# Raw weights of two quads in one tile: splits of 1024 columns, one accumulating transfer for both, and the output projection's transposes behind their unit

## The chip, the cores and the metric

The kernel runs on one core of a Trainium2 chip. The metric is the device time of one launch in microseconds (us), lower is better. The engines are called PE (TensorE: matmuls; PEld are its weight loads), DVE (VectorE), ACT (ScalarE), POOL (GpSimd) and SP (SyncE). Each runs its own instructions in order and waits for others by semaphores; transfers are issued by SP's and POOL's queues and land later.

## The reference

One layer of a hybrid decoder, for 256 positions of width 2048, all in float32. Cut to what matters here:

```python
def swiglu(h, w_gate, w_up, w_down):
    return (jax.nn.silu(h @ w_gate) * (h @ w_up)) @ w_down
...
        x = x + 0.5 * swiglu(rmsnorm(x, ffn1_norm[l]), ffn1_w_gate[l], ffn1_w_up[l], ffn1_w_down[l])
        h = rmsnorm(x, mix_norm[l])
        a_q, a_k, a_v, m_q, m_k, m_v, m_o, m_i, m_f = jnp.split(h @ w_in[l], split_idx, axis=-1)
...
        y_b = hm * jax.nn.sigmoid(m_o)
        x = x + jnp.concatenate([y_a, y_b], axis=-1) @ w_out[l]
        x = x + 0.5 * swiglu(rmsnorm(x, ffn2_norm[l]), ffn2_w_gate[l], ffn2_w_up[l], ffn2_w_down[l])
    return rmsnorm(x, final_norm)
```

Between them stand a differential attention (`y_a`) and an mLSTM (`hm`), both small. The FFN's inner width is 5632. Nearly all the time goes into `x @ w` with weights that are read once.

## The kernel before

**Products.** A float32 product is made of three matmuls of a faster, rounded type (fp32r). Each raw weight tile is split: ACT casts it to `wh` (L131), DVE subtracts that from the raw values to give the remainder `wl` (L132). The activations are split likewise. `mms` then issues, for each job, `wh` by the high part (L178) and `wh` by the low part (L179), and behind all jobs of the list `wl` by the high part (L181). Tiles `wh` and `wl` come from the pool `wsp`, four of each, so that ACT and DVE can run up to four tiles ahead of PE; splits have a high priority (AHEAD) and their order among themselves is the program's.

**Units.** `Paired` computes two output chunks of 512 columns, with weights `wa` and `wb`, in one unit. Of the contraction's 2048 (in tiles of 128 rows) the first `ns` "quads", each of two row tiles by two chunks, are multiplied by a scheme with seven products in place of eight; the remaining rows (`rest`) go by `plain` products, one tile of 128x1024 each. Quads are taken two at a time (`twos`). A quad's raw tile has three slots: one row tile of `wa` in slot 0 and both of `wb` in slots 1 and 2. The unit's stages are:

- `leading`: for each pair of quads it loads the raw tiles (L420 for `wa`, L205 for `wb`), splits slot 0 and multiplies (`part`, A1), and then DVE forms sums in place (L453). One pair later comes `second_sum`: the split and product of S1, and then slot 0 += slot 2. That sum is an accumulating transfer issued by POOL (L469), one for each quad; for the last of `twos`, and in units with `by_dma` off or three quads or fewer, it is a DVE addition (L471).
- `sums`: for each pair, the split and product of slot 0 (S2), then POOL adds the quad's second row of `wa` to it, which `late` has loaded through SP (L506, one transfer for each quad), and `bare` splits and multiplies the late tile itself. Then the same for S3 from slot 1.
- `second`: `both` (slots 0 and 2 of a quad, 128x1024 in one split) and the plain rows of `wa`; `third`: the plain rows of `wb`. `third` of a unit is run by `Chain` amid the next unit's `leading`.

Gate and up projections have `ns` = 5, in 20 units of both FFNs (pairs 2, 2, 1, so that two pairs of them take the transfer L469, four transfers a unit); the mixer's have 3 or 4, the down projections 3 or 2 with `by_dma` off, the output projection 3. Raw tiles of quads come from the pool `wr` (five tiles of one quad), plain and late ones from `wrp`.

In the split of a pair, each quad is split by itself, the two going to halves of one `wh` and one `wl`:

```python
                    for i, src in enumerate(srcs):
                        made = split_weights(src, t[0][:, i, :], t[1][:, i, :])
```

**Output projection.** Its input is `yT`, made by `y_transposes` (L1064): PE transposes `ya` (attention, in `weighted`) and `yb` (mLSTM, in `gate_out`) into `tr`, and ACT and DVE split them into `xt` or `xs`. The work is queued in `side` (one piece is run at each step, by `aside`) or in `pending` (run by `flush`). `second(gently=True)` is used in the first of the two output-projection units (c = 0): it runs one piece of `pending` at each step.

Program order, priorities and the tiles that come free set the order on each engine; the order of PE's matmuls in an FFN is the program's.

## Time and profile before

| what | value |
| --- | --- |
| median of 3 runs | 1776.93 us (1776.9 to 1777.61) |
| profiled execution, its own time | 1777.38 us |
| its span | 1775.3 us |
| granted TensorE clock | 0.999 |
| PE busy | 1758.5 us (99%) |
| DVE busy | 1605.0 us (90%) |
| ACT busy | 1263.6 us (71%) |
| POOL busy | 417.2 us (24%) |
| DMA moved | 427.08 MB, mean 241 GB/s |

A row of a timeline gives the start in us from the span's start, the duration in us, the engine, the line, the operation, what it writes and reads, the shape and how many stand in the row; in brackets the time for which the engine had been idle before, and what ended that. Where several instructions stand in one row, the duration is that from the first one's start to the last one's end. A row of groups ends in the busy time, the mean duration in ns, and the idle time just before with what ended most of it. A row of waits reads: who waited, at which line, for what; us in total, times, the longest one.

### The profile page before, as it was taken

What the parts mean: (1) busy time and instruction counts of PE and PEld (TensorE: products, weight loads), DVE (VectorE), ACT (ScalarE), POOL (GpSimd) and SP (SyncE); (2) the same over time, 40 slices, a digit from 0 to 9 for tenths busy, and PEclk for the clock granted to TensorE, in tenths of its full rate; (3) what the DMA queues carried; (4) which work ended last, traced back from release to release, by engine and by line L of the source; (5) the groups of instructions that cost most, each with busy time, mean ns of one, the idle gap of its engine ahead of it and who ended that gap; (6) DMA issues with size and microseconds to landing.
All of it is one profiled execution on the core that took longest, in us unless ns stands there. A gap on an engine that the chain in (4) does not pass through costs nothing. (4 is left out here: it accounts for less than half of the span.)

```text
span 1775.3 us, 24424 instructions
## 1 busy us (share of the span) xinstructions
PE 1758.5 (99%) x7942; PEld 1437.3 (81%) x7942; DVE 1605.0 (90%) x2168; ACT 1263.6 (71%) x1931; POOL 417.2 (24%) x614
## 2 busy tenths in 40 slices
PE   9999999999999999999999999999999999999998
PEld 7888888788888888987888788888888788888786
DVE  6989998999999999897788899999998999999998
ACT  7666676777677768776676677776676777677765
POOL 0022332332233311111121101122332333223310
PEclk9999999999999999999999999999999999999999
DMA  9787997998799876576776578897998999799874
GB/s 344 255 252 211 257 275 244 249 288 267 212 256 273 261 237 206 181 232 203 218 208 188 166 226 221 243 278 227 247 266 268 234 286 265 231 249 270 242 263 125
DMA packets 153296, 427.08 MB, mean 241 GB/s; under 512 B 17392, under 2 KB 18448, under 8 KB 152912
## 3 DMA queue, kind: packets, MB, share of 16 engines
q0 software_dynamic: 74192, 191.68, 42.8%
q1 hardware_dynamic: 77824, 231.76, 38.4%
q10 hardware_dynamic: 1152, 2.09, 0.3%
q8 instruction: 62, 1.02, 0.2%
q14 instruction: 66, 0.54, 0.1%
HBM read 349.56 MB, written 2.10 MB: 198 GB/s over the span
## 5 line engine op out<-in xcount | busy, mean ns | idle before, releaser
L131 ACT CAST wh<-raw 128x512 fp32r<-128x512 f32 (+2 forms) x865 | 587.1, 707 | 276.2 <-PE acc L179 84.6
L132 DVE TENSOR_TENSOR wl<-raw,wh 128x512 fp32r<-128x512 f32 (+2 forms) x865 | 661.6, 793 | 92.9 <-ACT wh L131 90.0
L132 DVE TENSOR_TENSOR wl<-rawp,wh 128x1024 fp32r<-128x1024 f32 (+3 forms) x316 | 373.9, 1197 | 25.8 <-ACT wh L131 21.4
L131 ACT CAST wh<-rawp 128x1024 fp32r<-128x1024 f32 (+3 forms) x316 | 322.5, 1033 | 60.1 <-PE acc L179 30.4
L178 PE MATMUL acc<-wh,xs 128*128 128x512 f32 (+2 forms) x924 | 358.6, 389 | 0.7 <-ACT us L477 0.5
L179 PE MATMUL acc<-wh,xs 128*128 128x512 f32 (+2 forms) x924 | 356.9, 387 | 0.0
L181 PE MATMUL acc<-wl,xs 128*128 128x512 f32 (+2 forms) x924 | 309.9, 389 | 1.2 <-DVE wl L132 1.1
L506 POOL DMA_DIRECT2D raw<-late x172 | 149.0, 1021 | 397.1 <-DVE wl L132 341.7
L178 PE MATMUL acc<-wh,xt 128*128 128x512 f32 (+2 forms) x592 | 228.7, 387 | 0.2 <-ACT wh L131 0.2
L178 PE MATMUL accn<-wh,xt 128*128 128x512 f32 (+1 forms) x576 | 227.6, 398 | 0.6 <-ACT accn L477 0.4
L179 PE MATMUL acc<-wh,xt 128*128 128x512 f32 (+2 forms) x592 | 227.8, 386 | 0.0
L179 PE MATMUL accn<-wh,xt 128*128 128x512 f32 (+1 forms) x576 | 224.0, 391 | 0.5
L453 DVE TENSOR_TENSOR raw<-raw 128x1024 f32<-128x1024 f32 (+1 forms) x172 | 206.6, 1216 | 0.1
L181 PEld LDWEIGHTS acc<-wl,xs 128*128 128x128 f32 x924 | 172.5, 188 | 41.5 <-DVE wl L132 7.2
L178 PEld LDWEIGHTS acc<-wh,xs 128*128 128x128 f32 x924 | 173.6, 188 | 36.1 <-ACT us L477 1.2
L179 PEld LDWEIGHTS acc<-wh,xs 128*128 128x128 f32 x924 | 173.6, 188 | 34.4 <-DVE xs L132 0.3
L181 PE MATMUL acc<-wl,xt 128*128 128x512 f32 (+2 forms) x592 | 165.3, 387 | 0.3
L181 PE MATMUL accn<-wl,xt 128*128 128x512 f32 (+1 forms) x576 | 161.3, 389 | 0.0
L178 PE MATMUL accn<-wh,xs 128*128 128x512 f32 (+1 forms) x392 | 153.2, 392 | 1.4 <-ACT wh L131 1.3
L179 PE MATMUL accn<-wh,xs 128*128 128x512 f32 (+1 forms) x392 | 151.9, 388 | 0.1
L469 POOL DMA_DIRECT2D raw<-raw x86 | 73.6, 873 | 307.0 <-DVE wl L132 293.7
L181 PE MATMUL accn<-wl,xs 128*128 128x512 f32 (+1 forms) x392 | 136.1, 389 | 0.1
(229 smaller groups left out, 2135.1 us busy)
## 6 DMA issues: line engine op xcount, KB each, us to landing
rawp<-in_wd_dram SPq DMA_DIRECT2D x88, 512.0 KB, 5.3
raw<-late POOLq DMA_DIRECT2D x170, 256.0 KB, 5.2
raw<-in_wu_dram POOLq DMA_DIRECT2D x80, 512.0 KB, 7.9
rawp<-in_wu_dram SPq DMA_DIRECT2D x74, 512.0 KB, 5.2
rawp<-in_wg_dram SPq DMA_DIRECT2D x70, 512.0 KB, 5.1
raw<-in_wd_dram POOLq DMA_DIRECT2D x44, 512.0 KB, 7.4
rawp<-in_win_dram SPq DMA_DIRECT2D x44, 512.0 KB, 4.6
raw<-raw POOLq DMA_DIRECT2D x86, 256.0 KB, 3.6
```

The costliest lines, as they stand in the source:

```text
L131: return (nc.scalar.copy(hi, src), nc.vector.tensor_tensor(out=lo, in0=src, in1=hi.bitcast(F32), op=ALU.subtract))
L132: nc.vector.tensor_tensor(out=lo, in0=src, in1=hi.bitcast(F32), op=ALU.subtract))
L178: nc.tensor.matmul(acc, lh, rh, start=first, stop=False, skip_group_check=on)
L179: nc.tensor.matmul(acc, ll, rh, start=False, stop=False, skip_group_check=on)
L181: nc.tensor.matmul(acc, lh, rl, start=False, stop=last, skip_group_check=on)
L453: nc.vector.tensor_tensor(out=raw[:, 0:2, :], in0=raw[:, 0:3:2, :], in1=raw[:, 1:2, :].to_broadcast([P, 2, n]), op=ALU.add)
L469: nc.gpsimd.dma_start(raw[:, 0, :], raw[:, 2, :], accum_op=ALU.add)
L506: nc.gpsimd.dma_start(self.raws[j][:, 0, :], lates[-1][1][:, i, :], accum_op=ALU.add)
```

## The change

- The pool `wr` holds tiles of two quads (`raw2`, two buffers) and of one quad (`raw1`, one buffer) in place of five tiles of one quad; the bytes are the same. `load` brings both quads' rows of `wa` in one transfer (512 KB) and each quad's of `wb` in one.
- A pair is split in one cast and one subtraction of 1024 columns. Its `wh` and `wl` stand where they stood.
- Slot 0 += slot 2 is one accumulating transfer of 512 KB for both quads (L478), and so is the addition of the late rows (L512); where DVE does the sum it is one instruction for both (L480).
- `mms` keeps its newest matmul, and in the first output-projection unit a piece of `pending` is issued behind that matmul (`tc.issue_after`). For the first attention head an empty piece goes into `side` ahead of its transposes, so that transposes of all heads run one step later.
- Spare loads (some plain tiles of the first unit) share one `raw2` tile.

The number of matmuls does not change, nor their order in the FFNs.

```diff
-    wr = ctx.enter_context(tc.tile_pool(name="wr", bufs=5))
+    wr = ctx.enter_context(tc.tile_pool(name="wr", bufs=2))
...
+    newest = []
     def mms(jobs):
...
-            nc.tensor.matmul(acc, lh, rl, start=False, stop=last, skip_group_check=on)
+            newest[:] = [nc.tensor.matmul(acc, lh, rl, start=False, stop=last, skip_group_check=on)]
...
+    def raw_tile(quads, n):
+        tag, bufs = ("raw2", 2) if quads == 2 else ("raw1", 1)
+        return wr.tile([P, quads, 3, n], F32, tag=tag, name=nm(tag), bufs=bufs)
...
-    def load(self, j):
+    def load(self, js):
...
-                self.queue.dma_start(raw[:, 0, :], self.wa[k // LK][:, k % LK, :])
-                load_pair(raw[:, 1:3, off:], self.wb, k, self.queue)
+                self.queue.dma_start(raw[:, :, 0, :], self.wa[k // LK][:, row:row + 2 * len(js) - 1:2, :])
+                for q in range(len(js)):
+                    load_pair(raw[:, q, 1:3, off:], self.wb, k + 2 * q, self.queue)
...
-    def split_two(self, srcs):
+    def split_two(self, src):
             with tc.high_priority(offset=AHEAD):
-                t = pair_tiles(wsp, "w", [P, 2, self.n])
-                if len(srcs) == 1 and len(srcs[0].shape) == 3:
-                    made = split_weights(srcs[0], *t)
-                else:
-                    for i, src in enumerate(srcs):
-                        made = split_weights(src, t[0][:, i, :], t[1][:, i, :])
-                splits.append(made)
+                t = [x[:, 0:src.shape[1], :] for x in pair_tiles(wsp, "w", [P, 2, self.n])]
+                splits.append(split_weights(src, *t))
             return t
...
-            t = self.split_two([self.raws[j][:, slot, :] for j in js])
+            t = self.split_two(self.twin[js[0]][:, :, slot, :])
...
-                        nc.gpsimd.dma_start(raw[:, 0, :], raw[:, 2, :], accum_op=ALU.add)
+                    nc.gpsimd.dma_start(raw[:, :, 0, :], raw[:, :, 2, :], accum_op=ALU.add)
...
-                    for i, j in enumerate(js):
-                        nc.gpsimd.dma_start(self.raws[j][:, 0, :], lates[-1][1][:, i, :], accum_op=ALU.add)
+                    nc.gpsimd.dma_start(self.twin[js[0]][:, :, 0, :], lates[-1][1][:, 0:len(js), :],
+                                        accum_op=ALU.add)
...
-                flush(1 if gently else 0 if i % 2 else None)
+                if gently:
+                    with tc.issue_after(newest[0].ins):
+                        flush(1)
+                else:
+                    flush(0 if i % 2 else None)
...
+        if h == 0:
+            side.append(lambda: None)
         side.append(functools.partial(y_transposes, [y[:, hb, :] for hb in range(NT)], 2 * h, gatt))
```

What this does to the order of instructions is seen in one gate-and-up unit on DVE, from the S1 split of its first pair to the S2 split of its second. Before (`raw_429`, `raw_430` are the first pair, `raw_436`, `raw_437` the second, `raw_442` the fifth quad; `rawp` is a plain tile of the unit before, `wl_456` and `wl_459` are S2):

```order
L132 TENSOR_TENSOR wl_441_2239<-raw_430_2183,wh_440_2238 128x512
L132 TENSOR_TENSOR wl_444_2256<-raw_442_2252,wh_443_2255 128x512
L132 TENSOR_TENSOR wl_446_2264<-raw_436_2218,wh_445_2263 128x512
L453 TENSOR_TENSOR raw_442_2252<-raw_442_2252 128x1024
L132 TENSOR_TENSOR wl_446_2264<-raw_437_2221,wh_445_2263 128x512
L132 TENSOR_TENSOR wl_449_2280<-raw_442_2252,wh_448_2279 128x512
L471 TENSOR_TENSOR raw_442_2252<-raw_442_2252 128x512
L132 TENSOR_TENSOR wl_452_2290<-rawp_450_2287,wh_451_2289 128x1024
L132 TENSOR_TENSOR wl_456_2312<-raw_429_2180,wh_455_2311 128x512
L132 TENSOR_TENSOR wl_456_2312<-raw_430_2183,wh_455_2311 128x512
L132 TENSOR_TENSOR wl_459_2328<-raw_436_2218,wh_458_2327 128x512
L132 TENSOR_TENSOR wl_459_2328<-raw_437_2221,wh_458_2327 128x512
```

And after, in the same unit (`raw2_420` is the first pair, `raw2_426` the second, `raw1_431` the fifth quad; `wl_445` and `wl_448` are S2, and the row of `sg` is the gate of the unit before, which stood there before as well):

```order
L132 TENSOR_TENSOR wl_430_2145<-raw2_420_2094,wh_429_2144 128x1024
L463 TENSOR_TENSOR raw2_426_2128<-raw2_426_2128 128x1024 x2
L132 TENSOR_TENSOR wl_433_2159<-raw1_431_2155,wh_432_2158 128x512
L463 TENSOR_TENSOR raw1_431_2155<-raw1_431_2155 128x1024
L132 TENSOR_TENSOR wl_435_2167<-raw2_426_2128,wh_434_2166 128x1024
L132 TENSOR_TENSOR wl_438_2180<-raw1_431_2155,wh_437_2179 128x512
L132 TENSOR_TENSOR wl_441_2190<-rawp_439_2187,wh_440_2189 128x1024
L480 TENSOR_TENSOR raw1_431_2155<-raw1_431_2155 128x512
L132 TENSOR_TENSOR wl_445_2212<-raw2_420_2094,wh_444_2211 128x1024
L382 SCALAR_TENSOR_TENSOR sg_413_2070<-acc_347_1754,rstd_52_360,sg_413_2070 128x512
L132 TENSOR_TENSOR wl_448_2225<-raw2_426_2128,wh_447_2224 128x1024
```

The first pair's S1 split now stands whole ahead of the sums of the second pair (before, one of those sums stood between its halves), and the DVE sum of the fifth quad stands behind the plain tile's split, not ahead of it.

On POOL, the same unit's transfers from the last load on, before:

```order
L205 DMA raw_442_2252<-in_wu1_dram 128x1024
L469 DMA raw_429_2180<-raw_429_2180 128x512
L469 DMA raw_430_2183<-raw_430_2183 128x512
L469 DMA raw_436_2218<-raw_436_2218 128x512
L469 DMA raw_437_2221<-raw_437_2221 128x512
L506 DMA raw_429_2180<-late_454_2309 128x512
```

and after:

```order
L207 DMA raw1_431_2155<-in_wu1_dram 128x1024
L478 DMA raw2_420_2094<-raw2_420_2094 128x2x512
L478 DMA raw2_426_2128<-raw2_426_2128 128x2x512
L512 DMA raw2_420_2094<-late_443_2209 128x2x512
L512 DMA raw2_426_2128<-late_446_2222 128x2x512
```

Where four transfers of one row stood, two of two rows stand, each behind the subtraction of the whole S1 pair.

In the output projection's first unit, PE's transposes of the second half of `yb`, before:

```order
L181 MATMUL acc_1901_9305<-wl_1934_9450,xs_1855_9115 128x512
L1064 MATMUL tr_1951_9533<-ident_107,yb_1929_9439 128x128
L1064 MATMUL tr_1958_9571<-ident_107,yb_1930_9442 128x128
L178 MATMUL acc_1901_9305<-wh_1936_9465,xs_1872_9177 128x512
L179 MATMUL acc_1901_9305<-wh_1936_9465,xs_1873_9178 128x512
L1064 MATMUL tr_1951_9533<-ident_107,yb_1929_9439 128x128 x3
L1064 MATMUL tr_1958_9571<-ident_107,yb_1930_9442 128x128 x2
```

and after:

```order
L183 MATMUL accn21_1908_9066<-wl_1911_9072,xt_1869_8894 128x512 x2
L1075 MATMUL tr_1912_9087<-ident_107,yb_1890_8998 128x128 x4
L180 MATMUL accn11_1881_8957<-wh_1915_9099,xt_1867_8884 128x512
L181 MATMUL accn11_1881_8957<-wh_1915_9099,xt_1867_8884 128x512
L180 MATMUL accn11_1881_8957<-wh_1915_9099,xt_1867_8884 128x512
```

They stood amid the leading phase's matmuls and now stand behind whole groups of matmuls, further down, the last head's (`yb_1891`) a group later still. The transposes of the first half of `yb` and of the last attention head moved the other way, to a place some 20 to 35 matmuls earlier; after:

```order
L183 MATMUL acc_1744_8400<-wl_1872_8902,xt_1331_6295 128x512 x2
L1075 MATMUL tr_1866_8879<-ident_107,yb_1853_8818 128x128
L1075 MATMUL tr_1868_8889<-ident_107,ya_1843_8776 128x128 x4
L183 MATMUL acc_1743_8399<-wl_1872_8902,xt_1331_6295 128x512
L1075 MATMUL tr_1866_8879<-ident_107,yb_1853_8818 128x128 x3
```

These stand in the third phase of the last unit of the input projection (`acc_1743`, `acc_1744` are its accumulators).

## The prediction

> **What bounds the kernel now.** I read the header of the page first, then the costliest groups with their shapes kept apart, then the table of waits, and last the timelines of single stretches, engine by engine.

> ```profile
> span 1775.3 us, 24424 instructions
> PE 1758.5 (99%) x7942; PEld 1437.3 (81%) x7942; DVE 1605.0 (90%) x2168; ACT 1263.6 (71%) x1931; POOL 417.2 (24%) x614
> ```

> TensorE is busy in 99% of the span. DVE and ACT, which make the two halves of every weight tile (ACT the rounded half `wh`, DVE the rest `wl`), are not the bound on average, so time saved on them is worth only what TensorE now waits for them. The question is thus where TensorE waits, and what the change makes late.

> ```profile
> L132 DVE TENSOR_TENSOR wl<-raw,wh 128x512 fp32r<-128x512 f32 x682 | 444.3, 686 | 33.0 <-ACT wh L131 31.0 <-PE acc L181 0.8
> L131 ACT CAST wh<-raw 128x512 fp32r<-128x512 f32 x682 | 399.6, 620 | 211.6 <-PE acc L179 68.9 <-DVE raw L453 54.4 <-PE acc L181 25.5
> L132 DVE TENSOR_TENSOR wl<-raw,wh 128x1024 fp32r<-128x1024 f32 x173 | 211.0, 1223 | 59.8 <-ACT wh L131 59.0
> L131 ACT CAST wh<-raw 128x1024 fp32r<-128x1024 f32 x173 | 181.9, 1054 | 63.6 <-PE accn L179 43.9 <-PE acc L179 15.7 <-DMA raw<-late 2.6
> L469 POOL DMA_DIRECT2D raw<-raw x86 | 73.6, 873 | 307.0 <-DVE wl L132 293.7 <-DVE mcol L385 13.3
> ACT wh L131 <- PE acc L179: 119.2, 187, 2.1
> PEld acc L181 <- DVE wl L132: 10.9, 30, 0.8
> ACT wh L131 <- DMA raw<-raw: 10.1, 22, 1.3
> ```

> Three things are to be seen. The casts mostly wait for TensorE to give a tile back (119.2 us in 187 waits): the splits run up to four tiles ahead. TensorE's own waits for the `wl` half are 10.9 us in 30 waits. And in 22 places ACT, which runs its instructions in order, waits for the accumulating transfer that adds one third of a raw tile onto another (10.1 us). In the span there are 20 units with five pairs of rows each (the gate and up projections of both FFNs), and each issues four such transfers of 256 KB; the other six of the 86 are in the mixer.

> **The change: merged splits.** 682 casts and 682 subtractions of 512 columns become 144 of each, and 269 pairs become one of 1024 columns each (173 to 441). By mean duration a pair costs 2 x 620 = 1240 ns on ACT and 1054 merged (269 x 186 ns = 50 us), and 2 x 686 = 1372 against 1223 on DVE (269 x 149 ns = 40 us). Instructions of one engine overlap at their ends, so both are upper bounds: the 1.28 us of two subtractions in a row (below) against 1.22 for one of 1024 gives 269 x 0.06 = 16 us for DVE. Where it hides: TensorE, 99% busy. What can come out of it is bounded by TensorE's waits on DVE's `wl` above, 10.9 us, and below by nothing. In six units a wait like this one stands at the `wl` of a plain tile (TensorE's weight loads):

> ```profile
> 412.51 0.30 PEld L181 LDWEIGHTS acc<-wl,xt 128*128 128x128 f32 x2 [0.50 <-DVE wl L132]
> ```

> A weight load every 0.23 us is the normal pace (two matmuls take 0.62 us where one takes 0.39, in rows below), so 0.5 us of waiting loses about 0.27. DVE came to that tile behind its sum L471; that sum now stands behind it. 6 x 0.27: I take -1.5 us. The other waits stand at tiles that the merge doesn't touch.

> The merge has a price as well: the first matmul of a pair now waits for the cast of 1024 columns, 1054 - 620 = 0.43 us later than for the first 512, which the four tiles of lead cover everywhere but in the next part.

> **The change: one accumulating transfer of 512 KB for two of 256 KB.** This is the part that decides. In each of the 20 units the fourth transfer L469 is issued in the last step of the leading phase, and the split of the sums S2 of the second pair waits for it. In a typical unit (POOL, then the landing of that transfer, then ACT, DVE and PE):

> ```profile
> 1311.70 0.84 POOL L469 DMA_DIRECT2D raw<-raw  x1 [0.89 <-DVE wl L132]
> DMA to landing us min/median/max: 3.5/3.5/3.5
> 1314.42 0.63 ACT L131 CAST wh<-raw 128x512 fp32r<-128x512 f32 x1
> 1315.25 0.62 ACT L131 CAST wh<-raw 128x512 fp32r<-128x512 f32 x1 [0.20 <-DMA raw<-raw]
> 1315.78 1.05 ACT L131 CAST wh<-late 128x1024 fp32r<-128x1024 f32 x1
> 1315.91 1.28 DVE L132 TENSOR_TENSOR wl<-raw,wh 128x512 fp32r<-128x512 f32 x2
> 1317.11 0.74 DVE L370 SCALAR_TENSOR_TENSOR sg<-acc,rstd,sg 128x512 f32<-128x512 f32 x1
> 1317.77 1.21 DVE L132 TENSOR_TENSOR wl<-late,wh 128x1024 fp32r<-128x1024 f32 x1
> 1317.53 0.39 PE L178 MATMUL acc<-wh,xs 128*128 128x512 f32 x1
> 1318.43 0.62 PE L181 MATMUL acc<-wl,xs 128*128 128x512 f32 x2
> 1319.79 0.62 PE L181 MATMUL accn<-wl,xs 128*128 128x512 f32 x2
> ```

> Before, the first half of this pair was cast at 1314.42, without a wait, and only the second half waited, 0.20 us, till 1311.70 + 3.5. Both then reached TensorE with time to spare: the subtractions ended at 1317.19, and TensorE used them at 1318.43.

> After, one transfer carries both halves. When is it issued? Like the fourth one, behind the subtraction of S1 of the second quad of that pair; the DVE work that stands ahead of it is the same but for the merges, which save some 0.2 us that a later start of the first of them takes away. So again 1311.70. How long does it take? No row shows an accumulating transfer of 512 KB. The nearest are two of 256 KB issued one behind the other (at 840.1 and 840.7: the first line below, and the least, middle and greatest time to landing in the second), and the loads of one and two rows by the same queue:

> ```profile
> L469 POOL DMA_DIRECT2D raw<-raw x2: 865/1014/1163, 840.1 to 840.7; - x2
> DMA to landing us min/median/max: 3.4/3.8/4.3
> raw<-in_wu_dram POOLq DMA_DIRECT2D x80, 512.0 KB, 7.9
> raw<-in_wg_dram POOLq DMA_DIRECT2D x80, 256.0 KB, 6.8
> 838.00:846.00 8.00, 8.00 (x37) 6.63 (x36) 7.01 (x11) 4.90 (x9) 1.90 (x3) 1.00 0.49 101
> 1300.00:1322.00 22.00, 22.00 (x98) 18.19 (x98) 21.80 (x29) 15.28 (x25) 7.71 (x9) 1.00 0.90 225
> ```

> The second of the two lands 0.6 + 4.3 = 4.9 us after the first issue, 1.4 us later than one alone (3.5). The loads differ by 7.9 - 6.8 = 1.1 us for the same doubling. I take 1.25 us, between them. The lower end is 0 (the transfer takes no longer); for the upper end I take 2.0 us, since the last two lines (windows; the last but one number is the busy share of the DMA engines) show 90% in this stretch against 49% around 840. [...]

> With 1.25 us: landing 1311.70 + 3.5 + 1.25 = 1316.45; the cast of 1024 ends at 1317.50 (TensorE wants it at 1317.53: just in time); the subtraction behind it ends 1.2 us later, at 1318.75 (wanted 1318.43: 0.3 late); then `sg`, 0.7 us, and the `wl` of the late tile, 1.2, ends at 1320.60, wanted at 1319.79. So TensorE stands 0.8 us in this unit. DVE has no idle time to make up for it: 21.80 of the 22 us of this stretch are busy. Behind it the splits catch up while TensorE stands, so the delay is paid once a unit.

> In other units the transfer is later already:

> ```profile
> 242.31 0.85 POOL L469 DMA_DIRECT2D raw<-raw  x1 [0.90 <-DVE wl L132]
> 246.69 0.62 ACT L131 CAST wh<-raw 128x512 fp32r<-128x512 f32 x1 [1.03 <-DMA raw<-raw]
> 248.61 1.22 DVE L132 TENSOR_TENSOR wl<-late,wh 128x1024 fp32r<-128x1024 f32 x1
> 248.14 0.39 PE L178 MATMUL acc<-wh,xs 128*128 128x512 f32 x1
> 250.40 0.61 PE L181 MATMUL accn<-wl,xs 128*128 128x512 f32 x2
> ```

> Here it takes 4.4 us. 1.25 more: cast 247.94 to 249.00 (wanted 248.14, 0.9 late), subtraction to 250.2, `sg` to 250.9, late `wl` to 252.1, wanted 250.40: 1.7 us. Going through the 20 units in the timelines I count twelve like the first, six like the second, and two with room. Sum: 12 x 0.8 + 6 x 1.7 = 19.8, +20 us. With 1.1 it is 12 x 0.65 + 6 x 1.55 = 17, with 1.4 it is 12 x 0.95 + 6 x 1.85 = 22.5, with 2.0 about 33, and with 0 nothing is late that isn't so now.

> The first pair's transfer of each unit has 0.8 us of room more, since its subtraction now stands ahead of the sums L453 of the next pair. In the mixer's units of four the split comes well behind the landing. The transfers L506 (now L512) are read only in the second phase. All these I cost at nothing.

> **The change: loads.** Bytes and packets stay the same; two loads of one row become one of two, ahead of the others. SP's queue keeps its own. The first row of a pair arrives later by what its second half takes, the second pair's `wb` rows at the same time as now. A single raw tile now comes free behind the last use of the quad before it, not of an older one; splits of a unit run ahead by more than that. 0 us, at worst 1 us in a unit.

> **The change: the output projection's transposes.** They stand behind the newest matmul of their unit, and one step later for the first head. In the stretch concerned (PE, then ACT and DVE):

> ```profile
> 989.63 0.30 PE L1064 MATMUL tr<-ident,ya 128*128 128x128 f32 x1 [0.55 <-DVE ya L385]
> 998.43 0.69 PE L1064 MATMUL tr<-ident,yb 128*128 128x128 f32 x2 [1.10 <-DVE xt L385]
> 1004.13 0.50 PE L181 MATMUL acc<-wl,xs 128*128 128x512 f32 x1 [0.32 <-DVE wl L132]
> 1004.83 0.50 PE L178 MATMUL accn<-wh,xt 128*128 128x512 f32 x1 [0.20 <-ACT wh L131]
> 991.03 1.28 ACT L385 ACT_TABLE_LOAD   x1
> 992.32 0.69 ACT L385 ACTIVATE og<-accn,rstd 128x512 f32<-128x512 f32 x1
> ```

> The four waits are 0.55 + 1.10 + 0.32 + 0.20 = 2.2 us, with the matmul's own pitch lost beside them some 3.4. That is the most there is to gain. What is late next: by the order of the changed program the first `yb` transposes stand about 4 us earlier than now, right behind the table load and `og` (1.28 + 2 x 0.69 us) and DVE's products; I expect a new wait of 1 to 1.5 us there. Net between -3.4 and 0; I take -1.5 us.

> **Sum.** The profiled execution took 1777.38 us, 2.1 over its span and 0.45 over the median of the runs. 1777.4 + 20 - 1.5 - 1.5 = 1794.4, against the median 1794; I round down to 1793, since the twelve units may hold a tenth or so of slack that the rows do not show.

> **Rivals.**
> - The transfer's delay is real but small (0.6 us or less): 6 x 0.9 + 12 x 0.15 = 7 us at 0.6, about 3 at 0.3, against the two gains of 3: 1774 to 1781, about the same, 1777. For it: the transfer of 512 KB pays its issue once. Against it: 4.9 us for a pair in a row.
> - Faster: DVE's relief. 16 us less DVE work in stretches where it is 99% busy (21.80 of 22) brings the subtractions forward, so that the cast's delay finds DVE waiting rather than behind, and the 10.9 us of waits for `wl` go too. It decides if DVE comes to the S1 subtraction 1 us or more earlier than now, so that the transfer is issued at 1310.7 instead of 1311.70 and lands as now: then 1777 - 8 - 2 = 1767. For it: that stretch of DVE. Against it: the start of its first merged subtraction waits for a cast of 1024.
> - Slower still: six raw loads of 1.5 MB leave in one burst when a pair's tile comes free and collide with the transfers, at 90% DMA share; with 2.0 us for the transfer +33: 1806.

> **How the numbers follow.** Forecast (1783 to 1802) 0.53; small delay 0.16 (0.03 of it slower by over 0.2%, 0.11 within, 0.02 faster); DVE's relief or a like gain 0.18; slower still 0.13. 0.2% (3.5 us) is about what a measurement of this kernel tells from no change. Slower: 0.53 + 0.13 + 0.03 = 0.69; same 0.11; faster 0.18 + 0.02 = 0.20. The range takes in the small delay, part of the relief and most of the last: 1770 to 1806.

> **What would show it.** In the changed profile: the median from issue to landing of `raw2<-raw2` at 512 KB, 4.7 to 4.9 us if right, 4.1 or less if the first rival holds; ACT's wait for that transfer at 20 to 35 us in place of 10.1; TensorE's waits for `wl` of a late tile up from near nothing to 0.8 to 1.7 us in 18 places, and its busy share down to about 98%; ACT's casts of 1024 from raw at 441, with a mean near 1054 ns; in the output projection a wait at the first `yb` transposes. The prediction is wrong if the transfer is issued over 0.5 us earlier than the fourth one was, or if the late tiles' `wl` is not what TensorE waits for behind it.

## The result and the profile after

The changed kernel takes 1851.23 us (median of 6 runs, 1848.02 to 1852.43) against 1776.91: a ratio of 1.0415, 95% interval 1.0402 to 1.0429. That is 74 us slower. Slower was forecast, but by 16 us only, and 1851 lies above the range. The page's header and engines:

```profile
span 1846.3 us, 23318 instructions
PE 1785.6 (97%) x7942; PEld 1442.7 (78%) x7942; DVE 1588.7 (86%) x1871; ACT 1232.9 (67%) x1659; POOL 340.0 (18%) x444
```

DVE and ACT did get less work, 1605.0 - 1588.7 = 16 us and 1263.6 - 1232.9 = 31 us, as the merges promise. TensorE's 7942 matmuls are the same, and it now stands where it did not before. The groups by shape and the waits that answer to those shown of before:

```profile
L132 DVE TENSOR_TENSOR wl<-raw,wh 128x1024 fp32r<-128x1024 f32 x441 | 536.1, 1220 | 174.2 <-ACT wh L131 171.0 <-PE acc L183 1.0 <-PE acc L181 0.4
L131 ACT CAST wh<-raw 128x1024 fp32r<-128x1024 f32 x441 | 462.7, 1051 | 288.7 <-DMA raw<-raw 76.0 <-DVE raw L463 62.9 <-PE accn L181 58.1
```

```profile
ACT wh L131 <- DMA raw<-raw: 76.0, 23, 5.5
ACT wh L131 <- DMA raw<-in_wg_dram: 49.8, 34, 5.9
PEld acc L180 <- ACT wh L131: 45.0, 28, 3.7
PEld acc L183 <- DVE wl L132: 28.5, 45, 1.9
```

And from the table of transfers (KB each, median us to landing):

```profile
raw<-raw POOLq DMA_DIRECT2D x43, 512.0 KB, 5.9
```

ACT's wait for the accumulating transfer went from 10.1 us to 76.0, in about as many places (22 and 23), and the transfer lands after a median of 5.9 us (3.6 before, for half the bytes). A new row has come to the front: TensorE's weight loads wait 45.0 us for the cast, `wh`, in 28 places. The same stage of a gate-and-up unit as in the prediction, by timelines of POOL, ACT and PE:

```profile
1343.06 1.22 POOL L478 DMA_DIRECT2D raw<-raw  x1 [7.72 <-DVE wl L132]
1348.34 1.21 POOL L478 DMA_DIRECT2D raw<-raw  x1 [4.06 <-DMA raw<-raw]
1354.37 1.04 ACT L131 CAST wh<-raw 128x1024 fp32r<-128x1024 f32 x1 [3.85 <-DMA raw<-raw]
1353.22 0.61 PE L183 MATMUL acc<-wl,xs 128*128 128x512 f32 x2
1355.47 0.50 PE L180 MATMUL acc<-wh,xs 128*128 128x512 f32 x1 [1.63 <-ACT wh L131]
```

The tile's own view gives the second transfer's time to landing:

```profile
DMA to landing us min/median/max: 6.0/6.0/6.0
```

Issue 1348.34 and 6.0 us give 1354.3; the cast of 1024 columns ends at 1355.4, and TensorE, which was ready at 1353.7, starts at 1355.47. Nothing stands ahead of the cast but the landing. The bracket behind the second L478 names the first one's landing; but its own subtraction (1.22 us from 1346.81) ended at the same time, and in another unit the second transfer left 4.3 us behind the first (at 381.82 and 377.49), while the quickest of the first transfers takes 5.0 us to land. So it does not wait for the first. In 19 of the 20 units TensorE stands at this place: 1.4 to 2.0 us in sixteen of them, 3.3 in one and some 0.5 in two.

What TensorE does next is the second part of the loss. Windows around that stall (the number behind the engines' busy times is the granted clock):

```profile
1353.60:1355.40 1.80, 0.24 (x2) 0.00 (x0) 0.00 (x0) 1.03 (x2) 0.00 (x0) 1.00 0.98 311
1355.40:1357.00 1.60, 1.46 (x5) 0.94 (x6) 1.55 (x2) 1.60 (x4) 0.02 (x1) 1.00 1.15 211
1357.00:1360.20 3.20, 3.20 (x9) 2.42 (x9) 3.20 (x5) 2.06 (x3) 2.00 (x2) 0.50 0.70 124
```

From 1357.0 to 1360.2 TensorE runs at a clock of 0.50: 9 matmuls in 3.2 us, where 14 fit. This follows some of the stalls, not all. Adding up the matmuls that start about 0.425 us behind the one before (0.227 at full clock) gives some 13 us lost in the changed kernel against 3.5 before, 2 us of it in the first 40 us. A stall that is no shorter, at 1498.28, has no half clock behind it:

```profile
1498.28 0.50 PE L180 MATMUL acc<-wh,xs 128*128 128x512 f32 x1 [1.71 <-ACT wh L131]
1353.62:1357.03 3.41, 1.71 (x6) 0.97 (x6) 1.58 (x2) 2.66 (x4) 0.05 (x1) 0.99 1.06 264
1493.51:1496.92 3.41, 3.06 (x14) 2.20 (x12) 1.55 (x2) 0.00 (x0) 1.17 (x1) 1.00 1.06 167
1496.92:1500.34 3.42, 2.00 (x8) 1.34 (x8) 2.08 (x3) 3.16 (x4) 0.55 (x1) 1.00 1.08 253
1500.34:1503.75 3.41, 3.28 (x15) 2.39 (x14) 3.41 (x5) 2.84 (x5) 1.50 (x2) 1.00 0.77 127
```

What tells most of them apart is in the clock and matmul records of the traces. In each profile the stretches of half clock (but for the one at the end) last 3.41 us or twice that, and their starts lie on one fixed grid of 3.41 us (in the changed kernel 339.8, 1357.0, 1435.5, 1452.6, 1694.9 and 1739.3). The windows above are cut on that grid: the first stall falls into one window, which is idle for half of it (1.70 us), and the next window runs at 0.50; the second stall is cut in two by the grid, idle 0.35 and 1.42 us, and nothing follows. Over all 16 profiles, without the first and last 40 us of each, 53 of the 57 full-clock windows idle for 1.7 us or more were followed by half clock, and 4 of the some 8000 others. The line at 1.7 us is this count's own, not a limit that the runs show: in the changed kernel's profile, cut exactly at the clock's records, windows idle for 1.70, 1.97 and 2.53 us were followed, and three with less (1.31, 1.64 and 1.68 us), while eight others with 1.32 to 1.66 us were not.

### The profile page after: what moved, and what is told of

It reads as the page before. It is cut to its first block, busy times and chain, and to the rows that moved or that the text cites. A ratio compares the mean times of both kernels' runs of the same rounds, so it can differ in the third digit from the quotient of the medians.

```text
span 1846.3 us, 23318 instructions
## 1 busy us (share of the span) xinstructions
PE 1785.6 (97%) x7942; PEld 1442.7 (78%) x7942; DVE 1588.7 (86%) x1871; ACT 1232.9 (67%) x1659; POOL 340.0 (18%) x444
## 5 line engine op out<-in xcount | busy, mean ns | idle before, releaser
L131 ACT CAST wh<-raw 128x1024 fp32r<-128x1024 f32 (+1 forms) x593 | 555.4, 943 | 388.2 <-DVE raw L463 94.8
L132 DVE TENSOR_TENSOR wl<-raw,wh 128x1024 fp32r<-128x1024 f32 (+1 forms) x593 | 636.9, 1085 | 181.6 <-ACT wh L131 177.2
L180 PE MATMUL acc<-wh,xs 128*128 128x512 f32 (+2 forms) x924 | 363.9, 394 | 34.0 <-ACT wh L131 33.9
L132 DVE TENSOR_TENSOR wl<-rawp,wh 128x1024 fp32r<-128x1024 f32 (+3 forms) x316 | 373.5, 1195 | 26.6 <-ACT wh L131 22.4
L131 ACT CAST wh<-rawp 128x1024 fp32r<-128x1024 f32 (+3 forms) x316 | 323.2, 1033 | 62.0 <-PE acc L181 34.5
L181 PE MATMUL acc<-wh,xs 128*128 128x512 f32 (+2 forms) x924 | 359.4, 389 | 0.0
L181 PE MATMUL acc<-wh,xt 128*128 128x512 f32 (+2 forms) x592 | 228.0, 386 | 0.0
L181 PE MATMUL accn<-wh,xt 128*128 128x512 f32 (+1 forms) x576 | 224.1, 392 | 0.7
L512 POOL DMA_DIRECT2D raw<-late x104 | 113.9, 1160 | 478.7 <-DVE wl L132 404.4
L181 PEld LDWEIGHTS acc<-wh,xs 128*128 128x128 f32 x924 | 175.1, 190 | 34.0
L180 PE MATMUL accn<-wh,xs 128*128 128x512 f32 (+1 forms) x392 | 155.1, 397 | 1.5 <-ACT wh L131 1.5
L181 PE MATMUL accn<-wh,xs 128*128 128x512 f32 (+1 forms) x392 | 154.0, 394 | 0.0
L183 PEld LDWEIGHTS acc<-wl,xt 128*128 128x128 f32 x592 | 109.8, 188 | 27.7 <-DVE wl L132 6.2
## 6 DMA issues: line engine op xcount, KB each, us to landing
rawp<-in_wd_dram SPq DMA_DIRECT2D x88, 512.0 KB, 5.6
raw<-in_wu_dram POOLq DMA_DIRECT2D x80, 512.0 KB, 8.2
rawp<-in_wu_dram SPq DMA_DIRECT2D x74, 512.0 KB, 5.1
rawp<-in_wg_dram SPq DMA_DIRECT2D x70, 512.0 KB, 6.0
raw<-late POOLq DMA_DIRECT2D x67, 512.0 KB, 5.9
raw<-in_wd_dram POOLq DMA_DIRECT2D x60, 512.0 KB, 6.8
rawp<-in_win_dram SPq DMA_DIRECT2D x44, 512.0 KB, 5.0
raw<-raw POOLq DMA_DIRECT2D x43, 512.0 KB, 5.9
```

The source lines that it names most:

```text
L131: return (nc.scalar.copy(hi, src), nc.vector.tensor_tensor(out=lo, in0=src, in1=hi.bitcast(F32), op=ALU.subtract))
L132: nc.vector.tensor_tensor(out=lo, in0=src, in1=hi.bitcast(F32), op=ALU.subtract))
L180: nc.tensor.matmul(acc, lh, rh, start=first, stop=False, skip_group_check=on)
L181: nc.tensor.matmul(acc, ll, rh, start=False, stop=False, skip_group_check=on)
L183: newest[:] = [nc.tensor.matmul(acc, lh, rl, start=False, stop=last, skip_group_check=on)]
L512: nc.gpsimd.dma_start(self.twin[js[0]][:, :, 0, :], lates[-1][1][:, 0:len(js), :], accum_op=ALU.add)
```

## The experiments

All start from the changed kernel, but for the two that are said to start from the kernel before. **Theory S**, as it became by the fifth run: what costs is that the merged S1 split lets no byte of the pair's addition start before the second half is subtracted. **Rivals**: the size of the transfer, the merged S2 split, the pairs' loads.

**The transfer's size alone.** One line:

```diff
-                    nc.gpsimd.dma_start(raw[:, :, 0, :], raw[:, :, 2, :], accum_op=ALU.add)
+                    for q in range(len(js)):
+                        nc.gpsimd.dma_start(raw[:, q, 0, :], raw[:, q, 2, :], accum_op=ALU.add)
```

> The changed kernel with one edit: slot 0 += slot 2 goes back to one accumulating transfer of 256 KB for each quad, both issued behind the merged S1 subtraction; all splits stay merged. Theory T (the 512 KB transfer is what costs: 5.9 us to landing instead of 3.5, some 2.3 us of stall in each of 19 units and half clock behind some of them): two transfers issued one behind the other land 4.9 us after the first issue, so about 1 us of each stall goes: 1851 - 19 to 25 = 1826 to 1832. Rival M (the merged S1 and S2 splits cost, not the transfer's size): unchanged within 5 us, 1846 to 1856. Rival L (the pair's loads cost): unchanged too.

Measured: 1874.09 us, ratio 1.0546 (1.0531 to 1.0560), slower by another 23 us, of which about half is half clock. No theory had this. The pair's two transfers in the same stage (their issues, their least, middle and greatest time to landing, and in a second view the cast behind them):

```profile
L479 POOL DMA_DIRECT2D raw<-raw x2: 845/1006/1167, 1372.4 to 1373.0; - x2
DMA to landing us min/median/max: 3.3/4.8/6.2
```

```profile
1379.22 1.04 ACT L131 CAST wh<-raw 128x1024 fp32r<-128x1024 f32 x1 [4.49 <-DMA raw<-raw]
```

From first issue to last landing 6.8 us, where the one transfer of 512 KB took 6.0. A transfer for both is thus the cheaper way to move both. The fault is not its size, but what has to wait until it is done.

**S1 and S2 quad by quad, with a transfer behind each half.**

```diff
-            t = self.split_two(self.twin[js[0]][:, :, slot, :])
+            if xi in (S1, S2):
+                t = self.split_each([self.raws[j][:, slot, :] for j in js])
+            else:
+                t = self.split_two(self.twin[js[0]][:, :, slot, :])
```

> The changed kernel with the splits of S1 and S2 of a pair made quad by quad again (two of 512 columns) and one accumulating transfer of 256 KB for each quad behind its own half; A1, S3, the late rows, the loads and the tiles stay merged. Theory T: the stalls at S2 of the second pair go altogether, 42 us and some 7 us of half clock; what is left over the kernel before are the late loads at the starts of units, some 25 us: 1798 to 1808. Rival L' (all of the loss hangs on the transfer, the late loads follow from it): 1775 to 1785. Rival C (the second half still comes too late since the loads collide): over 1820.

Measured: 1796.96 us, ratio 1.0107 (1.0093 to 1.0121): 54 us come back, and 20 stay.

**S1 alone.** The same edit with `(S1,)`; S2 stays merged and waits for both transfers.

> The changed kernel with S1 alone split quad by quad and one accumulating transfer of 256 KB behind each half; S2 stays one split of 1024 columns that waits for both transfers. Two transfers together landed 6.8 us after the first issue, one of 512 KB after 5.9, and alone 3.5. Theory S (what counts is when the first half of the pair's addition starts: the merged S1 puts it 1.7 us later, and then both halves' bytes are moved in a row): the last transfer lands as in the kernel before, and the merged S2 split costs at most 0.3 us a unit: 1795 to 1803, as with S1 and S2 both quad by quad. Rival M (the merged S2 split, which waits for both halves, costs most): 1820 to 1850.

Measured: 1798.60 us, ratio 1.0116 (1.0101 to 1.0131), as the run before. The merged S2 split, which waits for the last of both landings, costs nothing to be measured; the merged S1 split carries all 53 us. The transfers and ACT's wait for them in this run:

```profile
raw<-raw POOLq DMA_DIRECT2D x86, 256.0 KB, 3.7
```

```profile
ACT wh L131 <- DMA raw<-raw: 19.5, 18, 2.1
```

From the first issue of the second pair's two transfers to the last landing it takes 5.3 us in the median unit, here and in the kernel before, against 5.94 with one transfer: hardly more. But these 5.3 us begin 1.74 us earlier, behind the first half's subtraction (1309.97 and 1311.70 in the unit of the prediction). In the trace's packets the first half's bytes move from 1311.7 to 1313.1: the time from its issue to its first packet passes while DVE still works on the second half, and its bytes move ahead of the second half's.

**The same loss made in the kernel before.** If S is right, splits, sizes and tiles are not needed for it:

```diff
+                    raw, other = self.raws[js[1]], self.raws[js[0]]
+                    made = nc.gpsimd.dma_start(raw[:, 0, :], raw[:, 2, :], accum_op=ALU.add)
+                    with tc.issue_after(made.ins):
+                        nc.gpsimd.dma_start(other[:, 0, :], other[:, 2, :], accum_op=ALU.add)
```

> The kernel before with one edit: of each pair's two accumulating transfers (slot 0 += slot 2) the second quad's is issued first and the first quad's behind it, so that neither starts before the second half's S1 subtraction; splits, tiles, loads, sizes are those of before. Theory S (it is the start of the first half's bytes that counts): both land 6.8 us after the first issue as in the run with two transfers behind a merged S1, TensorE waits 1.5 to 2.4 us in 18 to 20 units and half clock follows some: 1810 to 1850. Rival M (the merged splits or the tiles of two quads are needed for the loss): 1777 to 1785.

Measured: 1813.92 us, ratio 1.0214 (1.0195 to 1.0234), 37 us slower than before by the order of two transfers alone. A unit of it (POOL, ACT, PE):

```profile
1333.56 0.85 POOL L468 DMA_DIRECT2D raw<-raw  x1 [1.18 <-DVE wl L132]
1334.09 1.18 POOL L470 DMA_DIRECT2D raw<-raw  x1
1339.83 0.62 ACT L131 CAST wh<-raw 128x512 fp32r<-128x512 f32 x1 [1.95 <-DMA raw<-raw]
1340.51 0.50 PE L178 MATMUL acc<-wh,xs 128*128 128x512 f32 x1 [0.98 <-ACT wh L131]
```

6.3 us from the first issue to the first cast, and TensorE waits. Theory S is shown, in both directions: the late start takes 37 of the 53 us on its own. The other 16 have no run of their own. As an estimate from the rows: TensorE starts 0.68 us behind the first cast's start here, with casts of 512 columns, and 1.10 us behind it in the changed kernel (0.42 in each of 20 units, 8 us); the clock is at 0.50 for 3.4 us here, without the program's end, and for 27 there (half of the difference, 12 us); and two transfers in a row land 0.3 us later than the one (6.2 and 5.9 in the median, 5 us the other way).

**No transfer for the second pair: DVE adds it.** The condition `js != self.twos[-1]` becomes `js == self.twos[0]`.

> The changed kernel, all splits merged, but slot 0 += slot 2 of the second pair by DVE (128x2x512, some 1.2 us) and not by a transfer. Theory S: the wait for the transfer goes (42 us and half clock behind it), DVE's 1.2 us a unit costs 0 to 15 us in a stretch where it is nearly always busy: 1797 to 1815. Rival (DVE is the next bound there): 1815 to 1840.

Measured: 1813.85 us, ratio 1.0202 (1.0185 to 1.0219), at the upper end of theory S: 37 us better than the change, 15 worse than S1 quad by quad. The likely price is DVE's 1.2 us a unit, where it is nearly always busy: TensorE's weight loads wait 35.3 us for `wl`, 26.9 with S1 quad by quad.

**Why 5.9 us and not 5.0?** The first pair's transfer lands after 5.0 us in 12 of the 20 units, the second's after 5.9 to 6.0 in 17. In the unit shown each moves its first packet 1.7 to 1.8 us behind its issue; the first then moves its packets in 3.0 us, the second in 3.8. Two things run beside the second: the late rows' addition L512, and a load of a plain tile by SP. The first try at holding L512 back used an edge between a split and the transfer, which moved nothing.

> The changed kernel with the first pair's transfer of the late rows (L512, 512 KB) held back behind the S2 split of the second pair, so that it no longer runs beside the transfer that this split waits for. Theory S with contention (5.96 us to landing for the second pair against 5.05 for the first, since L512 and a load of SP run beside it): landing near 5.4, 0.5 us less in each of 19 units, some half clock less: 1832 to 1843. Rival (the load of SP alone makes the difference, or the start): 1848 to 1853.

Measured: 1852.68 us, 1.0429 (1.0410 to 1.0448), with L512 3.5 us behind L478 as in the changed kernel: this run is the changed kernel once more, and says nothing on the question. The second try puts the first pair's L512 behind the second pair's on POOL itself:

```diff
+                        made = add_late(js, lates[-1][1])
+                        if len(self.twos) > 2 and js == self.twos[1]:
+                            with tc.issue_after(made.ins):
+                                add_late(*held)
```

> The changed kernel with the first pair's transfer of the late rows (L512) issued behind the second pair's on POOL, so that it cannot run beside the transfer L478 that the second pair's S2 split waits for. If L512 is what makes L478 land after 5.96 us and not 5.05: landing 5.0 to 5.5 and 10 to 18 us saved, 1833 to 1842. If the load of SP beside it is (a plain tile of 512 KB): landing 5.9, 1847 to 1854.

Measured: 1879.88 us, 1.0571 (1.0554 to 1.0589). Its timelines of POOL and of SP's queue, the landing of that L478, and a row of its waits:

```profile
1375.02 1.21 POOL L478 DMA_DIRECT2D raw<-raw  x1 [4.06 <-DVE wl L132]
1383.63 3.30 POOL L512 DMA_DIRECT2D raw<-late  x3 [7.39 <-DVE wl L132]
1376.54 0.33 SPq L228 DMA_DIRECT2D rawp<-in_wg_dram  x1
```

```profile
DMA to landing us min/median/max: 5.9/5.9/5.9
```

```profile
ACT wh L131 <- DMA rawp<-in_wg_dram: 29.3, 20, 2.6
```

L512 is now 8.6 us away, and the landing is still 5.9: it was not L512. SP's load of 512 KB, 1.5 us behind, is what is left beside it in these rows; taking that away was not tried, so that it is the cause is not shown. The run, slower than both of its ranges, has another wait that the changed kernel has not (1.0 us, once): in the last row, plain tiles come late, 20 times, since the tiles of late rows are given back later.

**Half clock.** Small matmuls into an accumulator that nobody reads, in the place of the stall:

```diff
+                    for _ in range(14):
+                        nc.tensor.matmul(idle[:, 0:P], ident_b, ident_b, start=True, stop=True)
```

> The changed kernel with 14 small matmuls (identity by identity, 128 columns, into a spare accumulator that nobody reads) ahead of the S2 products of the second pair in the 20 units of five quads, where TensorE stands 1.5 to 1.8 us: 14 x 0.11 = 1.5 us of work in a place where it waits anyway. Theory G (half clock, 0.50 for some 3 us behind a stall, comes from the stall itself): the granted clock goes from 0.991 to about 0.995 and 5 to 9 us are saved: 1842 to 1847. Rival (the clock drops for another cause): no slower, no faster, 1850 to 1856, with the half clock still there.

Measured: 1852.56 us, 1.0425 (1.0406 to 1.0444): no gain. They ran in about 0.9 us, not 1.5, so that 0.5 to 2.0 us of idleness stayed behind them in most units, and half clock cost some 12 us in place of 13. The run was too weak to tell the two apart. What bears on it is the count over the other 15 profiles of this case: of 65 stalls of 0.9 to 1.4 us 1 was followed by half clock within 6.5 us, of 46 of 1.4 to 1.9 us 6, of 61 longer ones 46 (by the starts of consecutive matmuls, less the usual 0.227 us, without the first and last 40 us). The windows on the grid sort them better (53 of 57, and 4 of some 8000 others): that the idle share of one window is what counts fits these counts, and no run set it by itself. At 1353.6 1.70 us of idleness in one window of 3.41, half of it, had half clock behind it.

**The 14 to 20 us that stay.** Everything quad by quad but the tiles and their load:

> The changed kernel with every split, sum and accumulating transfer quad by quad, as before; what stays of the change are the tiles of two quads (two and one buffer), their merged load, and the output projection's edit. Theory T with late loads: 1795 to 1805, about as the run with only S1 and S2 quad by quad, with waits of ACT for raw<-in_wg at 40 us or more. Rival L' (loads cost nothing by themselves): 1774 to 1780. If it is 10 us or more below the run with S1 and S2 quad by quad, the merged A1 and S3 splits or the DVE sum for both quads cost that much.

Measured: 1791.20 us, ratio 1.0077 (1.0064 to 1.0091), between its two ranges. So 14 us hang on tiles and loads; some 6 to 7 on the other merges. Some 10 of the 14 are lost at two places (4.4 and 5.5 us by the starts of the same matmuls, half clock included): the first gate-and-up unit behind the down projections, in each FFN. POOL and ACT there, in the kernel before and then in this run:

```profile
270.69 0.54 POOL L420 DMA_DIRECT2D raw<-in_wg_dram  x1 [2.54 <-DVE xs L132]
314.08 0.57 POOL L420 DMA_DIRECT2D raw<-in_wg_dram  x1 [6.69 <-DVE wl L132]
316.27 0.92 POOL L330 DMA_DIRECT2D xres<-part  x1
317.03 0.62 ACT L131 CAST wh<-raw 128x512 fp32r<-128x512 f32 x1 [0.22 <-PE acc L179]
319.13 0.62 ACT L131 CAST wh<-raw 128x512 fp32r<-128x512 f32 x1 [1.48 <-DMA raw<-in_wg_dram]
```

```profile
271.17 0.54 POOL L433 DMA_DIRECT2D raw<-in_wg_dram  x1 [1.72 <-DVE xs L132]
316.20 0.86 POOL L342 DMA_DIRECT2D xres<-part  x1 [8.26 <-ACT part L341]
316.84 0.83 POOL L433 DMA_DIRECT2D raw<-in_wg_dram  x1
317.57 1.18 POOL L207 DMA_DIRECT2D raw<-in_wu_dram  x2
324.37 2.71 ACT L131 CAST wh<-raw 128x512 fp32r<-128x512 f32 x5 [4.61 <-DMA raw<-in_wg_dram]
```

Two things are different. First, which quads come late. The kernel before loads the unit's five quads in order: one at 270.69, two at 291.84 and 292.97, and at 314.08 the fourth and the fifth; ACT casts three quads and then waits for the fourth, till 319.13. In this run the place that comes free first, at 271.17, is that of one quad (a load of 256 KB), and can only take the fifth quad, which is needed last; the first pair follows at 293.55, and the whole second pair at 316.84. ACT casts two quads and then waits, till 324.37. Second, the load stands behind the residual's addition in POOL's queue, where it stood ahead of it: 2.8 us later, 2.2 when the 0.55 us by which this run is behind there is taken off, with the pair's 1.5 MB to come and that addition running beside it. Three more runs looked at it. Loads of `wa` quad by quad, in the same tiles:

> Every split, sum and accumulating transfer quad by quad, as in the run that gave 1791, and the loads of wa quad by quad too; only the tiles of two quads with two buffers and one of one quad stay of the change, and the output projection's edit. Theory P (a tile of two quads is given back only behind its second quad's last use, so loads start late): about the same, 1786 to 1793. Rival Q (the merged load of wa, which brings the second quad's row ahead of the first quad's wb, is what is late): 1775 to 1781.

1795.76 us, 1.0101 (1.0086 to 1.0117), above both of its ranges: not the merged load, which is if anything the better. All tiles as slices of one, each free by itself:

> All splits, sums, accumulating transfers and loads quad by quad, as in the run that gave 1796, but all raw tiles are slices of one tile that is never given back, so that each quad's load waits only for that quad's own last reader (places as in the change: two pairs in turn, one fifth place). Theory P (tiles of two quads, given back only behind their second quad, make the loads late): most of the 18 us over the kernel before goes: 1776 to 1785. Rival (one place for the odd quad, which every unit needs, is what makes loads late): 1788 to 1797.

1789.64 us, 1.0071 (1.0055 to 1.0088): 6 us of 18 come back, so the later return of a tile is part of it and not most; the result lies in the range of the rival, that the one place for the odd quad makes loads late. POOL and ACT at the first of the two places (`ring` is the one tile):

```profile
315.15 0.57 POOL L442 DMA_DIRECT2D ring<-in_wg_dram  x1 [6.69 <-DVE wl L132]
317.34 0.91 POOL L350 DMA_DIRECT2D xres<-part  x1
320.77 0.62 ACT L131 CAST wh<-ring 128x512 fp32r<-128x512 f32 x1 [2.87 <-DMA ring<-in_wg_dram]
```

POOL's order is that of the kernel before, there and at the other place (1392.34 and 1394.52), and ACT still waits for the third quad. The two places still lose 3.3 and 2.2 us, without any half clock, of 4.4 and 5.5 with it. The same slices with the merges but S1's:

> The same slices and loads quad by quad, with S1 alone split quad by quad and A1, S2, S3, the late rows and the sum by DVE merged as in the change: the merges without the long transfer and without the tiles of two quads. Theory P and S together: 1775 to 1788. If merged splits gain by themselves, it is the fastest of all: under 1774.

1807.22 us, 1.0171 (1.0147 to 1.0194): a miss for all of its expectations, 9 us slower than the tiles of two quads with the same merges (and with the merged load). What the five quads' places cost is thus not settled. POOL's order is not most of it; that a place for one quad can only take the fifth fits the rows and the run with slices, but no run has lifted that alone, and why this last run is slow stays open.

**A1 and S3 merged, nothing else.**

> The run with every split, sum and transfer quad by quad (1791) with A1 and S3 of a pair merged; transfers and the sum by DVE stay quad by quad. The run that had besides these the late rows' transfer and the sum by DVE merged gave 1797. If the merged splits cost the 6 us: 1795 to 1799. If the merged sum by DVE in units of three quads does (128x2x512, which the S2 split of a pair waits for): 1789 to 1793. If merged splits gain: under 1788.

1793.12 us, 1.0088 (1.0073 to 1.0103), against 1.0077 (1.0064 to 1.0091) with none merged: the merged splits neither gain nor cost what can be told. The 4 us to 1796.96, again with overlapping intervals, are left for the merged transfer of the late rows and the merged sum by DVE together; they were not parted.

**The output projection's edit alone, in the kernel before.**

> The kernel before with the output projection's edit alone (transposes behind the newest matmul, an empty piece ahead of the first head's). By the prediction's term: -1.5 us, between -3.4 and 0: 1773.5 to 1777. Rival: the new wait at the first yb transposes outweighs the waits removed, +1 to +2: 1778 to 1779.

1775.66 us (median of 11), ratio 0.9992 (0.9983 to 1.0001): -1.3 us at the middle, not told from nothing by the whole time. At its own place it can be told: by the starts of the same matmuls, its profile gains 1.45 us on the kernel before between 970 and 1012. Twelve other profiles with the edit, which have other changes there too, gain 1.4 to 2.3, and the one without it 0.0. It was the fastest of all kernels tried, and no version clearly beats the kernel before.

## Why the prediction was wrong

- **The mechanism and its place were right.** The split of S2 of the second pair waits for the accumulating transfer, TensorE stands there in 19 of 20 units, once a unit, and the merged splits that save DVE 16 us gain nothing.
- **The step that failed is the landing, "I take 1.25 us".** The transfer lands 5.9 us after its issue, 2.4 more than the 3.5 of one alone, over even the upper end of 2.0. The pair of rows at 840 that gave 1.4 us came from a stretch with 49% of the DMA engines busy and no load beside; the first transfer of each unit, 5.0, agrees with it (4.9), the second, with SP's load beside, does not. And the issue came some 0.5 us later against TensorE's need than I had worked out (1348.34 against 1353.7 is 5.3 us ahead; 1311.70 against 1317.53 was 5.8).
- **By its own steps, with these two:** 0.5 + 1.15 = 1.65 us more than the 0.8 in each typical unit; measured is a stall of 1.4 to 2.0 us at the cast in most units and 1.8 to 2.8 us with the smaller ones behind it, so some 42 us in place of 20. Where the wait falls was off as well: at the cast (`wh`), 45.0 us, and not at the `wl` of the late tile, which I had latest.
- **A term was missing: the clock.** Half clock behind stalls takes about 10 us more than before (some 13 against 3.5). The prediction had read the clock at 0.999 and left it there. S1 quad by quad brings most of both back, 53 us.
- **"Loads: 0 us, at worst 1 us in a unit" failed.** The tiles and loads cost 14 us, mostly at two places, where ACT waits for the second pair's loads. The prediction asked when the single tile comes free, and not what it can hold; and it looked at bytes and room in the steady units and not at the first unit behind a down projection. The cause is in part open, as said above.
- **Merged splits, -1.5 us:** not found; A1 and S3 merged give +2 us, and the other merges some 4 us of loss, both with overlapping intervals. (The counts were 268 pairs and 146 single splits, for 269 and 144.)
- **The output projection, -1.5 us:** -1.3 us, with an interval that reaches to zero, and 1.45 us at its own place. Its new wait stands where it was expected, of the size expected (1 to 1.5 us), here in the changed kernel:

```profile
1012.54 0.30 PE L1075 MATMUL tr<-ident,yb 128*128 128x128 f32 x1 [1.11 <-DVE yb L397]
```

- **The sum:** 1851 - 1777 = 74, of which 53 by the merged S1 (in the profiled executions 48.5, some 40 of stalls and 9 of clock), 14 by tiles and loads (the output projection's edit among them), and 7 by the other merges.
- **The rival "slower still"** named 2.0 us and collisions with a pair's raw loads, and gave 1806: nearer in the landing (2.4), with less than half of the loss. In the unit shown no raw load runs beside the second transfer, only SP's plain one.
- **A slip in the rival "small delay":** at 0.6 us its six later units are 1.7 - 0.65 = 1.05 us late by its own working, not 0.9, so 8 us and not 7. Nothing hangs on it. Nor does any run show a delay of 0.6 us or less: the transfers of 512 KB landed after 5.0 us at the quickest and 5.9 in the median, 1.5 and 2.4 more than the 3.5 of one alone.

## What to carry to other kernels

A merge makes the whole wait for its last part: before two transfers are made one, or two splits one, look at what the first half was doing while the second was still being made. Price a longer wait by rows from the same stretch, with the same neighbours on the queues, and not from the nearest quiet one; and where stalls come near the lengths that had half clock behind them here (3 of 3 windows of 3.41 us with 1.70 us of idleness or more in the changed kernel), look at the clock behind them and add what it takes, here some 13 us. Where a tile's size changes, look at the seams between phases, not at the steady state alone: which tile comes free first there, and which data it can hold.
